# The modulation groups behind the first are made beside the attention instead of beside the branch projections

## The chip, the cores and the metric

The kernel runs on one core of one Trainium2 chip, as one program. The metric is device time in microseconds, from runs of the whole program. Engines are called PE (TensorE, matrix products), DVE (VectorE), ACT (ScalarE), POOL (GpSimd) and SP (the queue that issues nearly all loads).

## The reference, cut to what matters

Two layers act on 256 latent and 256 context tokens of 1024 features, all in float32. Of each layer:

```python
mod = jax.nn.silu(c) @ w_mod[l] + b_mod[l]          # latent; mod_c from c_ctx for the context
sh1, sc1, g1, sh2, sc2, g2 = jnp.split(mod[:, None, :], 6, axis=-1)
y_lat, y_ctx = token_mixers(x_lat * (1 + sc1) + sh1, x_ctx * (1 + csc1) + csh1, ...)
x_lat = layer_norm(alpha * x_lat + g1 * y_lat, ln1_g[l], ln1_b[l])
f_lat = expert_choice_ffn(x_lat * (1 + sc2) + sh2, ...)
x_lat = layer_norm(alpha * x_lat + g2 * f_lat, ln2_g[l], ln2_b[l])
```

`w_mod[l]` is 1024 x 6144. The token mixer has four branches: A, a gated delta rule over chunks of tokens in two directions; B, a difference of two softmax maps; C, grouped-query attention; D, attention with a window and a sink. Each branch's output is multiplied by `w_br`, gated by a sigmoid of 1024 logits per token, summed, and multiplied by `w_out`. The feed-forward has 16 experts that each choose 32 tokens per stream; its weights are 16 x 3 matrices of 1024 x 1024 per layer. The second layer computes latent tokens only behind its keys and values.

## The kernel before, in words

**Modulation.** The six modulation vectors of a layer are made in three groups of two. `mod(l, g)` (L220) is a generator. For each of eight blocks k of 128 rows it loads 128 x 2048 weights (1 MB) by `wload` from SP into one of the three buffers of the pool `wp`, and issues four products (L237) of 128 x 32 by 128 x 512, one for each strip of 32 rows of the PSUM tile `ps_mod`; the eight blocks add up there. The four products stand under `tc.high_priority()`. It yields after each block. After the eighth, the sums are copied, transposed (`ps_mt`, L245) and added to the biases. `ps_mod` is one of the two tiles of the PSUM pool `pa`, from which the attention's scores (`score_ps`), layer 0's state products of the scan and later sums also come. Group (0, 0) is made at the start. Groups (0, 1), (0, 2) and (1, 0) belong to layer 0's mixer, (1, 1) and (1, 2) to layer 1's; their results are used first behind the merge of the branches (gates and norms) and in the next layer.

**Mixer.** `run` takes the steps of `ORDER = "PMBIV"`: P projects branch A and convolves, M makes A's chunk matrices, B projects the three attention branches (`bcd_project`, seven groups of 256 columns: a 1 MB load from `w_in`, a split of each weight into a high and a low part on ACT, DVE and POOL, and three passes of products per token tile into `ps_n`, at L311 to L313), I inverts A's triangles (`a_invert`: a long run on DVE, then products `ps_y` L655 and `ps_z`), V prepares values. Then come A's scan over eight steps, the attention of D, C and B in eight units (`attention`), the gate logits of the branches in `SPILL` (`gates`, `ps_gate`, ended by a tanh on ACT, L1123), the merge with the other branches' gates, the output projection, and the experts (`moe`). Weight loads of `w_mod`, `w_in` (branch and gate), `w_br` and `w_out` all go through `wp`.

**What sets the order.** Nobody writes the order on the engines by hand. A planner lays out every engine's instructions before the run, by a model of their costs: an instruction is placed when its operands and a buffer are free by that model, and among those ready the one that stands earlier in the program goes first (products under `high_priority` before all others). An instruction far down in the program can so be placed early. At run time each queue keeps that order and waits by semaphores.

In step B the generators take turns:

```python
def all_mods():
    it = (x for m in mods for x in self.mod(*m))
    while next(it, True) is None:
        for _ in range(2):
            next(it, None)
        yield
```

One turn is three blocks; `all_of(all_mods(), self.bcd_project(l, bp))` puts one turn ahead of each projection group. Layer 0 has 24 blocks in eight turns, layer 1 has 16 in six.

Of the kernel before, what the change touches and what calls it, by code (L numbers as in the profile page):

```python
# [27 lines left out]
# columns of the packed constants  # L28
# [57 lines left out]
# rows of the packed per-layer vectors (each of 128 elements)  # L86
R_BMOD, R_L1G, R_L1B, R_L2G, R_L2B, R_CONV, R_C, R_CC, NROW = 0, 48, 56, 64, 72, 80, 110, 118, 126
# columns of the packed per-layer small vectors
# [3 lines left out]
class Net:  # L92
# [16 lines left out]
    def rsqrt(self, out, x, n, tag, scale=1.0, eps=EPS):  # L109
        """out[128, n] = (x * scale + eps) ** -0.5"""  # L110
# [12 lines left out]
    def wload(self, src, shape, pool=None):  # L123
        """one streamed weight tile [128, a, b]"""
        w = (pool or self.wp).tile([P, 2048], F32, tag="w", name="w")
        v = w[:, :shape[0] * shape[1]].rearrange("p (a b) -> p a b", a=shape[0])
        self.nc.sync.dma_start(v, src)
        return v

    def split(self, w, n):  # L130
        """hi/lo parts of a streamed weight tile [128, 8, n]: lists over k of [128, n]"""
# [13 lines left out]
    def hilo(self, h, x, w, j):  # L145
        """w = h + x, h of 12 bits"""
# [8 lines left out]
    def rowbcast(self, dst, col):  # L155
        """dst [128, 1024] (every partition) = the vector held as columns col [128, 8]; two vectors: in turns of 32 partitions"""
# [16 lines left out]
    def setup(self):  # L173
# [36 lines left out]
        # silu of both conditioning vectors, padded to a column tile  # L210
# [9 lines left out]
    def mod(self, l, g):  # L220
        """modulation vectors 2g and 2g+1 of layer l, as columns"""
        nc = self.nc
        ps = self.pa.tile([P, 512], F32, tag="s", name="ps_mod")
        for k in range(8):
            src = self.a["w_mod"][l, k * P:(k + 1) * P, g * 2048:(g + 1) * 2048]
            if (l, g) == (0, 0) and k % 2:
                # at the start the weights' parts lend their tiles
# [27 lines left out]
    def all_of(*gens):  # L255
        """what the generators do, in turns"""
# [10 lines left out]
    def make_h(self, src, scl, shf):  # L267
        """src [128, 4 tiles, 1024] natural -> self.hp, transposed; scl/shf[w]: [128, 8] columns"""
# [24 lines left out]
    def h_tile(self, t):  # L293
        """both parts of the activations of token tile t: lists over k of [128, 128]"""
# [5 lines left out]
    def mm_h(self, ps, wh, wl, n0):  # L300
        """ps [128, 512 - n0] = weights.T @ activations of the tokens from n0 on"""
# [5 lines left out]
    def mm3(self, ps, lh, ll, rh, rl, nk=8):  # L307
        """ps = sum over k of (lh+ll).T @ (rh+rl), in three passes"""
# [7 lines left out]
    def a_inputs(self, l, st):  # L316
        """the projections for the decays, natural"""
# [9 lines left out]
        # the transposed keys' tile serves as scratch  # L327
# [8 lines left out]
    def a_project(self, l, st):  # L336
        """short convolution over q, k, v"""
# [5 lines left out]
        # natural k, v [tok, t, (h d)]; q is needed for a while only  # L343
# [4 lines left out]
        # transposed: [d, h, tok]  # L348
# [5 lines left out]
        def conv_tile(ci, hi, lo, c0):  # L354
            n0 = 256 if (ci < 2 and l == 1) else 0       # queries of the context are not needed
# [18 lines left out]
            # twice the silu; the factor is taken out where the result is scaled  # L374
# [19 lines left out]
        # l2 norms (of twice the silu)  # L394
# [23 lines left out]
    def a_gates(self, l, st):  # L418
        """log decays, their cumulative sums and the factors made of them"""
# [4 lines left out]
        # tiles that are filled later on serve as scratch  # L424
        Nm = A["N"] = pl.tile([P, 32, 64], F32, name="a_N")       # stack = (t, d, h)
# [16 lines left out]
        # log1p(e) = 2 atanh(s), s = e / (2 + e) <= 1/3  # L442
# [14 lines left out]
        # half of beta, for v carries a factor of two; beta itself for k  # L457
# [4 lines left out]
        # cumulative sums along the chunks, in the order of each scan: rows (head), tokens along the row;  # L462
        # the backward scan's tokens are reversed within their tile
# [11 lines left out]
        # G and G_last - G  # L475
# [10 lines left out]
        # as columns: [tok, (G, G_last - G), t, (d h)]  # L486
# [13 lines left out]
        # exp(G_last) on the partitions of the state: [d, (dir, chunk in the scan's tiles), h]  # L500
# [7 lines left out]
        # the backward rows once more, in the order of the tokens  # L508
# [6 lines left out]
        # exp(G), exp(G_last - G); beta exp(G)  # L515
# [13 lines left out]
    def a_mats(self, l, st):  # L529
        """per chunk: -(beta k k^T decay) (lower triangles) and (q k^T decay)^T"""  # L530
# [6 lines left out]
        pT = A["pT"] = pl.tile([P, 8 * nq, 64], F32, name="a_pT")      # stack = (query tile, d, h)  # L537
        nb = p1.tile([P, 4, 8], F32, name="a_nb")
        nc.vector.tensor_scalar_mul(nb, bt.rearrange("p t d h -> p t (d h)"), -1.0)
        for t in range(4):  # L540
# [16 lines left out]
            # row of -beta for the backward direction  # L557
# [27 lines left out]
    def a_invert(self, l, st):  # L585
        """R[s, c] = ((I - N)^-1)^T for the forward direction, (I - N)^-1 for the backward one"""
# [9 lines left out]
        # one 32 x 32 block per partition: F[(rb, s), j, i] = N[i, j]  # L596
        F = p1.tile([P, 32, 32], F32, tag="i_F", name="i_F")
        nc.vector.transpose(F, Dg.rearrange("p s j -> p j s"))
        T = p1.tile([P, 32, 32], F32, name="i_T")          # T[r, k], row-major
# [6 lines left out]
        def view(ap, off, dims):  # L606
            """ap: [128, n] flat; dims: (step, count)"""
# [3 lines left out]
        for r in range(1, 16):  # L611
            # rows 16 b + r, b = 0, 1
            i0 = view(Ff, r, [(16 * 33, 2), (0, r), (32, r)])                 # N[16b+r, 16b+q]  (b, k, q)
            i1 = view(Tf, 0, [(16 * 33, 2), (1, r), (32, r)])                 # T[16b+q, 16b+k]
# [3 lines left out]
        # T21 = T22 N21 T11 for the halves of 16  # L618
        Y = p1.tile([P, 16, 16], F32, name="i_Y")          # Y[j, i] = (T22 N21)[i, j]
        for i0, ni, nm in ((0, 8, 8), (8, 4, 16), (12, 4, 16)):  # L620
            # (i, j, m): T[16+i, 16+m] * N[16+m, j]
# [6 lines left out]
        for k0, nk in ((0, 8), (8, 8)):  # L628
            # (i, k, j): Y[i, j] * T[j, k], j >= k0
# [466 lines left out]
    def attention(self, l):  # L1096
# [3 lines left out]
        for i, (_, unit) in enumerate(jobs):  # L1100
            cur, nxt = nxt, (jobs[i + 1][0]() if i + 1 < len(jobs) else None)
            unit(*cur)
# [650 lines left out]
```

## Time and profile before

| | us |
|---|---|
| timed runs, median of 3 | 2188.01 (2185.98 to 2192.87) |
| profiled execution, span from first to last instruction | 2171.3 |
| PE busy in the span | 1849.2 (85%) |
| PE weight loads busy | 1199.7 (55%) |
| DVE busy | 955.9 (44%) |
| ACT busy | 503.8 (23%) |
| POOL busy | 350.6 (16%) |
| bytes moved | 553.92 MB, mean 255 GB/s |

For the profiled execution the span is what is given; its total outside the span is not recorded. Busy times of an engine are unions over its instructions. Matrix products are pipelined, so that one that shows 0.28 us may follow the one before it by 0.12. An instruction's idle time ahead of it is put down to what released it last. The PE clock is shown as a share of 2.4 GHz; its two levels are 1.2 and 2.4 GHz, and a stretch's number is a mean.

### The profile page before, as it was taken

The page shows a single profiled execution, that of the slowest core. Times are in us where ns is not written, and L with a number is a line of the kernel's source. Part 1 is how long each engine was busy: PE and PEld are TensorE (multiplying, and loading weights), DVE is VectorE, ACT ScalarE, POOL GpSimd, SP SyncE. Part 2 cuts the span into 40 slices and gives each one's busy share as a digit, 9 for nine tenths or more (in the row PEclk, how much of TensorE's full clock was granted, in tenths as well). Part 3 has the DMA queues.
Part 4 walks back from the last instruction along what each step waited for, and adds up shares of the span by engine and source line. Part 5 has one row for each costly group of instructions (what it writes and reads, how often), then busy time and mean ns, then how long its engine had stood idle before and what let it go on. Part 6 is the DMA issues. An engine that isn't in the chain of part 4 may idle for free. (4 is left out here: it accounts for less than half of the span.)

```text
span 2171.3 us, 33547 instructions
## 1 busy us (share of the span) xinstructions
PE 1849.2 (85%) x13730; PEld 1199.7 (55%) x13730; DVE 955.9 (44%) x2126; ACT 503.8 (23%) x1038; POOL 350.6 (16%) x380
## 2 busy tenths in 40 slices
PE   6898899989999899988797898899899886676665
PEld 2676778867788555322222376778889542232221
DVE  3859547773226424221121486977755430110102
ACT  2332116752222111000000332246543100000000
POOL 1151330012532000000000125330264000000000
PEclk9999999998999899999999999999999896777767
DMA  7445413117333589999999655302487899999996
GB/s 290 161 170 194 156 36 108 54 59 260 110 126 137 211 335 350 409 409 409 409 409 409 239 194 182 130 24 96 134 271 265 323 408 409 409 409 409 409 409 274
DMA packets 200181, 553.92 MB, mean 255 GB/s; under 512 B 16222, under 2 KB 83164, under 8 KB 194396
## 3 DMA queue, kind: packets, MB, share of 16 engines
q1 hardware_dynamic: 190960, 538.56, 65.6%
q10 hardware_dynamic: 9068, 13.23, 1.7%
q8 instruction: 108, 1.77, 0.3%
q14 instruction: 45, 0.37, 0.1%
HBM read 541.25 MB, written 10.49 MB: 254 GB/s over the span
## 5 line engine op out<-in xcount | busy, mean ns | idle before, releaser
L1458 PE MATMUL ps_gu<-w,xgT 128*32 128x256 f32 (+1 forms) x1632 | 241.2, 533 | 69.5 <-DMA w<-in_w_gate_e_dram 35.5
L149 POOL TENSOR_TENSOR wl<-w,wh 128x1024 fp32r<-128x1024 f32 x62 | 154.1, 2486 | 884.1 <-DMA w<-in_w_in_dram 504.2
L1458 PE MATMUL ps_gu<-we,xgT 128*32 128x256 f32 (+1 forms) x1440 | 204.1, 512 | 38.8 <-DMA we<-in_w_up_e_dram 24.3
L1458 PEld LDWEIGHTS ps_gu<-w,xgT 128*32 128x32 f32 (+1 forms) x1632 | 78.8, 134 | 212.1 <-issue 83.0
L1500 DVE TENSOR_TENSOR y<-ps_dn,g2r 32x512 f32<-32x512 f32 (+1 forms) x128 | 70.9, 554 | 259.0 <-PE ps_dn L1489 257.5
L311 PE MATMUL ps_gate<-hh,wh 128*128 128x512 f32 (+1 forms) x512 | 179.8, 351 | 0.4 <-ACT wh L148 0.4
L313 PE MATMUL ps_gate<-hh,wl 128*128 128x512 f32 (+1 forms) x512 | 179.5, 351 | 0.0
L312 PE MATMUL ps_gate<-hl,wh 128*128 128x512 f32 (+1 forms) x512 | 179.4, 350 | 0.0
L148 ACT CAST wh<-w 128x1024 fp32r<-128x1024 f32 x124 | 129.6, 1049 | 179.2 <-PE ps_gate L312 77.3
L1458 PEld LDWEIGHTS ps_gu<-we,xgT 128*32 128x32 f32 (+1 forms) x1440 | 63.1, 128 | 167.3 <-DMA we<-in_w_up_e_dram 62.1
L1489 PE MATMUL ps_dn<-w,eaT 128*32 128x256 f32 (+1 forms) x896 | 119.1, 522 | 32.5 <-DMA w<-in_w_down_e_dram 26.8
L1468 ACT ACTIVATE eth<-ps_gu 128x512 f32<-128x512 f32 (+1 forms) x32 | 15.7, 491 | 518.4 <-PE ps_gu L1458 518.4
L311 PE MATMUL ps_n<-wh,hh 128*128 128x256 f32 x400 | 116.7, 292 | 7.3 <-DVE c_v L861 3.1
L312 PE MATMUL ps_n<-wl,hh 128*128 128x256 f32 x400 | 115.8, 290 | 8.2 <-POOL wl L149 8.2
L1471 DVE SCALAR_TENSOR_TENSOR eac<-eth,ps_gu 128x512 f32<-128x512 f32 (+1 forms) x32 | 17.7, 554 | 235.1 <-PE ps_gu L1458 235.1
L149 DVE TENSOR_TENSOR wl<-w,wh 128x1024 fp32r<-128x1024 f32 x62 | 85.9, 1385 | 72.9 <-ACT wh L148 72.6
L313 PE MATMUL ps_n<-wh,hl 128*128 128x256 f32 x400 | 115.9, 290 | 0.0
L1489 PE MATMUL ps_dn<-we,eaT 128*32 128x256 f32 (+1 forms) x640 | 93.4, 512 | 15.6 <-DMA we<-in_w_down_e_dram 11.1
L311 PEld LDWEIGHTS ps_gate<-hh,wh 128*128 128x128 f32 x512 | 99.4, 194 | 11.4 <-ACT wh L148 0.8
L312 PEld LDWEIGHTS ps_gate<-hl,wh 128*128 128x128 f32 x512 | 99.2, 194 | 10.8
L313 PEld LDWEIGHTS ps_gate<-hh,wl 128*128 128x128 f32 x512 | 99.0, 193 | 10.8 <-DVE wl L149 0.2
L1470 DVE SCALAR_TENSOR_TENSOR eth<-eth,ps_gu 128x512 f32<-128x512 f32 (+1 forms) x32 | 17.7, 554 | 193.3 <-ACT eth L1468 193.3
(453 smaller groups left out, 3591.2 us busy)
## 6 DMA issues: line engine op xcount, KB each, us to landing
w<-in_w_gate_e_dram SPq DMA_DIRECT2D x75, 1024.0 KB, 13.2
w<-in_w_down_e_dram SPq DMA_DIRECT2D x72, 1024.0 KB, 12.7
w<-in_w_up_e_dram SPq DMA_DIRECT2D x62, 1024.0 KB, 13.9
we<-in_w_up_e_dram SPq DMA_DIRECT2D x120, 512.0 KB, 13.4
w<-in_w_in_dram SPq DMA_DIRECT2D x54, 1024.0 KB, 5.2
we<-in_w_down_e_dram SPq DMA_DIRECT2D x108, 512.0 KB, 14.0
we<-in_w_gate_e_dram SPq DMA_DIRECT2D x96, 512.0 KB, 13.9
w<-in_w_mod_dram SPq DMA_DIRECT2D x44, 1024.0 KB, 5.0
```

Source lines behind the costliest of these rows:

```text
L148: nc.scalar.copy(h, w)
L149: (nc.gpsimd if j else nc.vector).tensor_tensor(x, w, h.bitcast(F32), op=OP.subtract)
L311: nc.tensor.matmul(ps, lh[k], rh[k], start=(k == 0), stop=False)
L312: nc.tensor.matmul(ps, lh[k], rl[k], start=False, stop=False)
L313: nc.tensor.matmul(ps, ll[k], rh[k], start=False, stop=(k == nk - 1))
L1458: nc.tensor.matmul(ps[M * q:M * q + M, :NF], xg[e // 4][:, 2 * kk + k, e % 4, :], w[k][:, q * NF:(q + 1) * NF], start=(kk == 0 and k == 0) ...
L1468: nc.scalar.activation(th, pss[0][:, :NF], AF.Tanh, scale=0.5)
L1470: nc.vector.scalar_tensor_tensor(th, th, 1.0, pss[0][:, :NF], op0=OP.add, op1=OP.mult)
L1471: nc.vector.scalar_tensor_tensor(ac, th, 0.5, pss[1][:, :NF], op0=OP.mult, op1=OP.mult)
L1489: nc.tensor.matmul(py[M * q:M * q + M, :NF], av[:, fc % nj, fc // nj, :], w[k][:, q * NF:(q + 1) * NF], start=(fc == 0), stop=(fc == 7))
L1500: nc.vector.tensor_tensor(ys[w][32 * e4:32 * e4 + 32, q * NF:(q + 1) * NF], py[o:o + 32, :NF], g2r[o:o + 32, q * NF:(q + 1) * NF], op=OP.mult)
```

## The change

The call of `all_mods()` leaves step B. The generator is handed to `attention`, which takes one turn (three blocks) after each of its eight units, and what is left behind the last. The products, loads and their sizes stay the same. The diff also strips comments and docstrings, which are left out here.

```diff
-    def attention(self, l):
+    def attention(self, l, fill):
         B = self.B
         jobs = self.attn_gqa(l, 3, B["dqk"], B["dv"], True) + self.attn_gqa(l, 2, B["cqk"], B["cv"], False) + self.attn_diff(l)
         nxt = jobs[0][0]()
         for i, (_, unit) in enumerate(jobs):
             cur, nxt = nxt, (jobs[i + 1][0]() if i + 1 < len(jobs) else None)
             unit(*cur)
+            next(fill, None)
+        self.all_of(fill)
...
                     elif step == "B":
-                        self.all_of(all_mods(), self.bcd_project(l, bp))
+                        self.all_of(self.bcd_project(l, bp))
...
-                self.attention(l)
+                self.attention(l, all_mods())
```

## Rows read from the trace of the kernel before

**Rows 1.** the page: 40 slices, transfer rate, modulation loads (KB, us to landing).

```profile
PE   6898899989999899988797898899899886676665
GB/s 290 161 170 194 156 36 108 54 59 260 110 126 137 211 335 350 409 409 409 409 409 409 239 194 182 130 24 96 134 271 265 323 408 409 409 409 409 409 409 274
...
w<-in_w_mod_dram SPq DMA_DIRECT2D x44, 1024.0 KB, 5.0
```

**Rows 2.** stretches: length, each engine's busy time (instructions), PE clock, DMA share, GB/s.

```profile
123.00:255.00 132.00, 119.74 (x1037) 99.52 (x1035) 94.61 (x180) 31.26 (x54) 41.48 (x80) 0.99 0.54 185
255.00:280.00 25.00, 17.88 (x345) 13.52 (x344) 13.46 (x26) 5.64 (x11) 12.10 (x15) 0.80 0.17 54
280.00:345.00 65.00, 63.77 (x680) 50.13 (x680) 33.53 (x73) 14.93 (x25) 16.67 (x19) 1.00 0.23 78
345.00:470.00 125.00, 119.74 (x804) 101.70 (x804) 105.37 (x337) 93.51 (x277) 7.68 (x3) 0.99 0.15 52
1320.00:1340.00 20.00, 14.82 (x127) 10.32 (x124) 8.04 (x18) 2.73 (x3) 8.23 (x19) 0.74 0.49 167
1480.00:1562.00 82.00, 73.06 (x591) 66.55 (x589) 67.45 (x166) 52.06 (x127) 17.21 (x7) 0.99 0.35 119
```

**Rows 3.** tile ps_gate (min/median/max ns, first and last start), then ACT's timeline.

```profile
L1123 ACT ACTIVATE th<-ps_gate x16: 576/598/612, 277.6 to 500.3; 128x512 f32<-128x512 f32 x16
...
342.44 0.59 ACT L1123 ACTIVATE th<-ps_gate 128x512 f32<-128x512 f32 x1
...
382.43 0.60 ACT L1123 ACTIVATE th<-ps_gate 128x512 f32<-128x512 f32 x1
...
408.89 0.60 ACT L1123 ACTIVATE th<-ps_gate 128x512 f32<-128x512 f32 x1 [0.30 <-PE ps_gate L313]
```

**Rows 4.** DVE's timeline (start, us): the inversion's last copies, layers 0 and 1.

```profile
213.91 0.28 DVE L666 COPY a_N<-i_Tn 32x256 f32<-32x256 f32 x1
...
1400.55 0.28 DVE L666 COPY a_N<-i_Tn 32x256 f32<-32x256 f32 x1
```

**Rows 5.** tiles ps_n (layer 0) and ps_y (layers 0, 1): first and last start.

```profile
L313 PE MATMUL ps_n<-wh,hl x224: 277/281/469, 123.6 to 254.8; 128*128 128x256 f32 x112
...
L655 PE MATMUL ps_y<-i_Rn,a_N x128: 191/224/257, 255.4 to 269.8; 32*32 32x32 f32 x128
...
L655 PE MATMUL ps_y<-i_Rn,a_N x128: 191/224/257, 1415.0 to 1426.8; 32*32 32x32 f32 x128
```

**Rows 6.** PE's waits (total, times, longest us), 40 to 340, 1205 to 1440.

```profile
PE ps_z L677 <- DVE i_YT L658: 7.1, 1, 7.1
...
PE ps_mod L237 <- DMA w<-in_w_mod_dram: 3.6, 4, 1.6
...
PE ps_mod L237 <- DMA w<-in_w_mod_dram: 7.4, 3, 5.2
```

**Rows 7.** PE's timeline: the long wait ahead of a modulation product, layer 1.

```profile
1330.12 1.93 PE L237 MATMUL ps_mod<-w,silc 128*32 128x512 f32 x8 [5.18 <-DMA w<-in_w_mod_dram]
```

**Rows 8.** modulation products, 40 to 500 (busy, mean ns, idle), then 123 to 260.

```profile
L237 PE MATMUL ps_mod<-w,silc 128*32 128x512 f32 x192 | 26.4, 624 | 3.7 <-DMA w<-in_w_mod_dram 3.6
...
L237 PE MATMUL ps_mod<-w,silc x128: 592/605/617, 124.6 to 236.9; 128*32 128x512 f32 x128
```

**Rows 9.** SP's queue (start, us from first to last of the merged issues).

```profile
220.17 8.61 SPq L127 DMA_DIRECT2D w<-in_w_mod_dram  x3
234.02 91.58 SPq L127 DMA_DIRECT2D w<-in_w_in_dram  x6
```

**Rows 10.** PE's timeline: two products of 512 columns in a row.

```profile
86.04 0.39 PE L311 MATMUL ps_a<-hh,wh 128*128 128x512 f32 x1
86.27 0.40 PE L312 MATMUL ps_a<-hl,wh 128*128 128x512 f32 x1
```

**Rows 11.** score tiles ps_sc: layer 0's first products; layer 1's row maxima.

```profile
L1019 PE MATMUL ps_sc<-kA,qT x32: 277/388/500, 348.0 to 403.4; 128*128 128x256 f32 x16, 128*128 128x512 f32 x16
...
L974 DVE TENSOR_REDUCE mx<-ps_sc x32: 666/680/692, 1434.8 to 1543.4; 128x1 f32<-128x512 f32 x32
```

## The prediction

> **What bounds the kernel now.** The span is 2171.3 us. First the forty slices [rows 1]: TensorE (PE) is busy nearly throughout, and the transfers run at 409 GB/s only in slices 17 to 22 and 33 to 39, where the experts' weights stream. So each layer has a mixer stage, bound elsewhere, and a feed-forward stage paced by transfers. The change touches the mixer; the feed-forward starts when that ends, so I carry a shift over whole.
>
> Then the stages [rows 2], with idle read as length minus busy. From 123 to 255 (attention projections, with modulation steps between) PE is idle for 12.3 of 132 us, in the inversion 7.1 of 25, in the scan 1.2 of 65, in layer 0's attention 5.3 of 125. PE stays full in scan and attention because a reserve is drawn on: the gate products of the spilled branches, later in the program, are pulled forward. Their first tile of sixteen is evicted at 277.6, the last at 500.3, the sixth at 342.44 [rows 3].
>
> Third, what the scan waits for. The inversion's VectorE part ends with the copy at 213.91, but its first product, ps_y, starts at 255.4, behind the last projection product of 254.8 [rows 4, 5]. PE takes the projections first. In layer 1 the copy is at 1400.55 and ps_y at 1415.0. So the projections' PE time holds up branch A by up to 41 and 14 us.
>
> Fourth, the waits [rows 6]: modulation products waited 3.6 us for transfers in layer 0 and 7.4 in layer 1, one wait 5.2 long, before the product at 1330.12 [rows 7]; around it, 1320 to 1340, the granted clock averages 0.74 [rows 2], a part of the time at 1.2 instead of 2.4 GHz. ps_z waited 7.1 us for VectorE, and the clock from 255 to 280 is 0.80.
>
> **What the change removes.** A step is one 1 MB load and eight records (four products, each recorded twice): 192 records, 24 steps, busy 26.4 us, or 1.1 each [rows 8]. 16 of layer 0's steps (128 records) lie between 124.6 and 236.9: 17.6 us of PE, and I count all 3.6 of waits with them. The eight earlier ones lie in the convolution; I count half of them, 4 us, as felt, because PE waits for VectorE there. The projections would end at 254.8 - 17.6 - 3.6 - 4 = 230. Layer 1 has 16 steps, 17.6 us, with its 7.4 of waits.
>
> **Where the steps go.** Not simply into the attention. The planner runs an instruction as soon as operands and a buffer are free, earlier program lines first; the gate weights, which stand behind the attention, were loaded from 234.02 on, directly behind the last modulation load of the 220.17 row [rows 9]. On that queue the modulation loads now come after the seventh projection load and before the gate loads, and their products keep the highest priority. They need one of three weight buffers. A projection group takes (131 - 17.6 - 3.6)/7 = 15.7 us, and its buffer is free about when its products begin, so the buffers of the last three groups come free some 47, 31 and 16 us before the projections end. A buffer turns round in about 7 us (5.0 to land [rows 1], 1.1 for the products, about 1 for the issue; an estimate from those rows): 2, 4 and 5 steps, 11 in all. They push the projections' end to 230 + 12 = 242. ps_y then starts 13 us earlier, with the inversion's copy (213.91) no limit.
>
> The 13 steps left run at the rate of transfers: 1.05 MB take 2.6 us at 409 GB/s, or 3.6 at the 290 of the first slice, where the first group's weights were streamed and the start is counted in [rows 1]; I take 2.8, nearer the first, 36 us, until about 278. So they fill inversion and scan, and the gate loads start near 275 instead of 234. Queued behind them on SP are those gate loads and nothing else that is urgent; ScalarE's and GpSimd's splits of gate weights follow. A gate tile is 24 products, 0.23 us apart in the same 512-column shape [rows 10]: 5.6 us. By the attention's start (13 us earlier than before), three tiles instead of six would be done, at one in 14 us as before; 17 us of them fall later, where PE is also full. The step count is constant, so moving is worth nothing by itself; only idle PE time and half clock are won.
>
> **Layer 0, the sum.** Waits for modulation loads: -3.6. The 7.1 of ps_z, which steps can fill: -7.1 to 0, taken -5, for steps arrive one in 2.8 us. Half clock, 25 x (1 - 0.80) = 5.0: -5 to 0, taken -3.5. New waits on streamed loads, a kind that the trace does not show: nearest are 3.6 in 24 steps and 7.4 in 16 (0.15 to 0.46 each), so 2 to 6 for 13 steps, or less than nothing if slack meets them; I take +3, with the scan's state products in it, which share a PSUM pool with the modulation sums. The hole in the reserve: gates filled 6 x 5.6 = 34 of the 86 us up to 342, 39%, and steps fill 1.1 in 2.8, the same; the first gate's load and split after them, +2; between 0 and 34. Sum -7.
>
> **Layer 1, the sum.** Waits -7.4, half clock 20 x (1 - 0.74) = 5.2, taken -4; new waits +2. In this layer all scores use the two PSUM tiles of one pool, and a modulation sum holds one of them for its eight loads. The attention's first scores may meet the last steps for some 20 us: 0 to 6 (32 scores lie between 1434.8 and 1543.4 [rows 11], one in 3.4 us), taken +1.5. Sum -8.
>
> Moved waits and the rest cancel. Span 2171.3 - 15 = 2156. No total of the profiled execution is given; the median of the timed runs, 2188.0, is 16.7 above the span, and I keep that: 2173.
>
> **A rule against PE as the bound.** In attention PE shows 119.7 busy of 125, its weight loads 101.7 [rows 2]. The Trainium skill ("Perfetto Trace Analysis", Identifying the Most-Contended Engine) says that matmul busy time does not measure headroom and that weight-load time does. By it layer 0 leaves 125 - 101.7 = 23 us of room for the steps, which is rival 3. The trace speaks against it so far: gates lay ready, yet one tile took from 382.43 to 408.89 to come through.
>
> **Rivals.** 1: the work merely changes place. New waits eat what the old ones give back; within 0.3%, about 2188. For it: PE idle in scan and attention is small. Against: the 5.2 us wait and the two half-clock stretches are whole gaps.
>
> 2: slower. The moved loads take the three weight buffers early, but their sums wait for their place among the scores; then no gate weights can be loaded through scan and half the attention. Six tiles, 34 us, that filled the time up to 342 are missing, PE idles there and pays them after the attention: +34 - 3.6. Layer 1 pays up to 10 of its 8 x 24 x 0.115 = 22 us of gates (half the columns) and gets 12 back. 2188 + 30 - 2 = 2216. It decides if the last modulation load of layer 0 is issued after the first score (348.0 in [rows 11]). For it: one buffer pool serves all, and loads stand ahead of the gates. Against: in [rows 9] instructions far behind the attention were pulled up without waiting for their turn, and nothing else wants the score pool before the scan.
>
> 3: attention has room, because only the weight loads bind PE, 101.7 of 125 us. Then steps and displaced gates vanish into it: layer 0 -23 - 3.6, layer 1 82 - 66.6 = 15 [rows 2] and 7.4: -49, 2139. For: 15 us or more of free weight-load time in each. Against: the gate tile above.
>
> **Chances.** Forecast 0.48, rival 1 0.22, rival 2 0.20, rival 3 0.10. The forecast's own range is 2160 to 2183. The range reaches toward rivals 2 and 3 and covers the hole's price up to half: 2152 to 2208. 0.3%, 6.6 us, is about what a measurement tells from no change: faster 0.55 (nearly all of the forecast, and rival 3), same 0.23, slower 0.22.
>
> **What would show it.** Modulation products from about 185 on, none between 70 and 160; ps_y near 242 and, in layer 1, near 1400; no 5 us wait for a modulation load as at 1330; the first gate tile evicted after 290, with about thirteen tiles left when the attention starts, against ten; the clock in the inversion above 0.80. The prediction is wrong if the products run during the scores, if scan or attention gains more than 10 us of idle PE, or if ps_y hardly moves.

## The result and the profile after

The kernel after takes 2275.9 us (median of 4 runs, 2268.0 to 2276.2) against 2187.0 (2182.3 to 2192.9) for the kernel before: ratio 1.041, 95% interval 1.038 to 1.044. The forecast was 2173, its range ended at 2208. The profiled span grew from 2171.3 to 2274.3, by 103 us; it is 89 in the medians, because the profiled execution of before was among its shorter ones. Places in the span are compared by the profiles, totals by the medians.

The page of after, forty slices: PE's busy tenths, its granted clock, the transfer rate [rows 1].

```profile
PE   6898769889899799989787788789889896676665
PEclk9989659999999899999999998969999897786877
GB/s 277 56 57 56 20 20 252 188 171 150 231 111 118 170 250 342 399 409 409 410 409 409 288 64 49 75 67 237 163 248 258 255 409 409 409 409 408 409 409 260
```

Slices 2 to 6, 57 to 341 us, move 20 to 57 GB/s where before moved 36 to 194. PE's tenths fall to 7 and 6 in slices 5 and 6, and the clock with them. The experts' slices are as they were. So the loss is in the mixers, and in layer 0 it begins with a lack of transfers. The next view, windows, shows the scan and the attention of layer 0 [rows 2] (length, busy us of PE, PEld, DVE, ACT, POOL, PE's clock, DMA share, GB/s):

```profile
255.00:320.00 65.00, 45.05 (x535) 41.86 (x532) 28.24 (x68) 3.66 (x8) 9.75 (x16) 0.50 0.00 1
320.00:330.00 10.00, 6.10 (x24) 4.44 (x24) 3.08 (x6) 5.38 (x12) 0.00 (x0) 0.50 0.27 105
330.00:470.00 140.00, 125.71 (x863) 88.44 (x864) 101.60 (x343) 87.69 (x267) 2.68 (x1) 0.95 0.56 198
```

From 255 to 330 the clock is 0.50, the lower level of 1.2 GHz for the whole stretch; PE is idle for 20 of the 65 us up to 320, in which next to nothing is moved (1 GB/s). SP's queue says why (start, us from first to last of the merged issues; it answers [rows 9]):

```profile
198.25 30.13 SPq L127 DMA_DIRECT2D w<-in_w_mod_dram  x3
...
346.46 22.83 SPq L127 DMA_DIRECT2D w<-in_w_mod_dram  x8
...
382.42 24.02 SPq L127 DMA_DIRECT2D w<-in_w_mod_dram  x8
...
435.58 10.53 SPq L127 DMA_DIRECT2D w<-in_w_mod_dram  x5
449.17 17.47 SPq L127 DMA_DIRECT2D w<-in_w_in_dram  x4
```

Three modulation loads take the three weight buffers by 228. The fourth can start only when a buffer comes free, at 346, and all gate loads stand behind the last one: the first gate weights are asked for at 449.17, at 234.02 before. What kept the buffers is in the tiles: the modulation sums, the gate tiles evicted [rows 3], layer 0's row maxima, and layer 1's [rows 11].

```profile
L237 PE MATMUL ps_mod<-w,silc x192: 592/592/617, 345.3 to 455.7; 128*32 128x512 f32 x192
...
L1125 ACT ACTIVATE th<-ps_gate x16: 586/599/600, 473.7 to 564.7; 128x512 f32<-128x512 f32 x16
...
L974 DVE TENSOR_REDUCE mx<-ps_sc x64: 404/548/692, 334.2 to 460.8; 128x1 f32<-128x256 f32 x32, 128x1 f32<-128x512 f32 x32
...
L974 DVE TENSOR_REDUCE mx<-ps_sc x32: 665/682/693, 1497.5 to 1633.0; 128x1 f32<-128x512 f32 x32
```

And layer 0's row maxima before:

```profile
L974 DVE TENSOR_REDUCE mx<-ps_sc x64: 399/544/693, 348.9 to 461.9; 128x1 f32<-128x256 f32 x32, 128x1 f32<-128x512 f32 x32
```

The first sum starts at 345.3, 14 us after the first score (331.4), though its first three loads had been issued by 228. The sums got their tile of the scores' pool in the order of the program, among the scores (with a tile from another pool, in e1 below, they start at 235.7). The gates, of which six tiles were evicted by 342 before, all come after 473. The attention, from its first maximum to its last, takes 126.6 us (before 113.0) in layer 0 and 135.5 (108.6) in layer 1.

The end of each layer's mixer, by the last product of the branch outputs (before, then after; min/median/max ns, first and last start):

```profile
L312 PE MATMUL ps_br<-ol,bh x64: 387/397/792, 463.4 to 653.7; 128*128 128x512 f32 x64
...
L312 PE MATMUL ps_br<-ol,bh x64: 278/283/579, 1547.1 to 1656.9; 128*128 128x256 f32 x64
```

```profile
L312 PE MATMUL ps_br<-ol,bh x64: 387/397/628, 564.8 to 717.9; 128*128 128x512 f32 x64
...
L312 PE MATMUL ps_br<-ol,bh x64: 278/283/415, 1651.2 to 1755.7; 128*128 128x256 f32 x64
```

Layer 0 ends 64.2 us later. From there to the same place in layer 1 it is 1037.8 us against 1003.2, 34.6 more, and 4.2 come after. These two lengths are the yardstick below. Kernels whose layer 0 is untouched end it between 652.7 and 654.0. The 64.2 can be split once more, by the windows from 40 us to that end (before, then after):

```profile
40.00:653.90 613.90, 569.60 (x3999) 454.51 (x4000) 359.23 (x786) 224.45 (x478) 170.77 (x183) 0.96 0.38 128
```

```profile
40.00:718.10 678.10, 599.90 (x3999) 488.93 (x4000) 357.41 (x787) 226.98 (x478) 171.39 (x183) 0.89 0.35 116
```

The same 3999 products are busy for 30.3 us more, at a mean clock of 0.89 instead of 0.96, and idle time grows from 44.3 to 78.2 us, by 33.9.

### The profile page after: what moved, and what is told of

The parts are those of the page before. It is cut to its first block, busy times and chain, and to the rows that moved or that the text cites. A ratio compares the mean times of both kernels' runs of the same rounds, so it can differ in the third digit from the quotient of the medians.

```text
span 2274.3 us, 33570 instructions
## 1 busy us (share of the span) xinstructions
PE 1899.0 (83%) x13730; PEld 1251.2 (55%) x13730; DVE 957.7 (42%) x2126; ACT 506.1 (22%) x1038; POOL 350.9 (15%) x380
## 5 line engine op out<-in xcount | busy, mean ns | idle before, releaser
L311 PE MATMUL ps_gate<-hh,wh 128*128 128x512 f32 (+1 forms) x512 | 175.2, 342 | 1.3 <-ACT wh L148 1.3
L1460 PEld LDWEIGHTS ps_gu<-we,xgT 128*32 128x32 f32 (+1 forms) x1440 | 62.7, 128 | 171.9 <-DMA we<-in_w_up_e_dram 66.2
L312 PE MATMUL ps_n<-wl,hh 128*128 128x256 f32 x400 | 121.2, 303 | 19.1 <-POOL wl L149 19.1
L311 PE MATMUL ps_n<-wh,hh 128*128 128x256 f32 x400 | 121.2, 303 | 10.4 <-DVE c_v L861 3.7
L1472 DVE SCALAR_TENSOR_TENSOR eth<-eth,ps_gu 128x512 f32<-128x512 f32 (+1 forms) x32 | 17.8, 555 | 196.6 <-ACT eth L1470 196.6
## 6 DMA issues: line engine op xcount, KB each, us to landing
we<-in_w_up_e_dram SPq DMA_DIRECT2D x120, 512.0 KB, 13.6
```

The costliest lines, as they stand in the source:

```text
L311: nc.tensor.matmul(ps, lh[k], rh[k], start=(k == 0), stop=False)
L312: nc.tensor.matmul(ps, lh[k], rl[k], start=False, stop=False)
L1460: nc.tensor.matmul(ps[M * q:M * q + M, :NF], xg[e // 4][:, 2 * kk + k, e % 4, :], w[k][:, q * NF:(q + 1) * NF], start=(kk == 0 and k == 0) ...
L1472: nc.vector.scalar_tensor_tensor(th, th, 1.0, pss[0][:, :NF], op0=OP.add, op1=OP.mult)
```

## The experiments

All at a glance. "First gate" is the first gate product of layer 0, "layer 0" its mixer's end against 653.7, "layer 1" the way from there to layer 1's against 1003.2; us, of one profiled execution each. The ratio is of the times, to before. What a profile differs by beyond the two columns comes behind layer 1's mixer (-0.1 to 11.5 us). In e14, whose layer 1 is that of before, layer 1 differs by 3.2; differences of that size say nothing.

| kernel | median | ratio (95%) | first gate | layer 0 | layer 1 |
|---|---|---|---|---|---|
| before | 2182 to 2187 | 1 | 256.6 | 0 | 0 |
| after | 2275.9 | 1.041 (1.038 to 1.044) | 460.6 | +64.2 | +34.6 |
| e1 sums in the other PSUM pool | 2210.9 | 1.014 (1.011 to 1.018) | 386.0 | +25.7 | +5.7 |
| e2 behind the projections | 2206.4 | 1.012 (1.009 to 1.016) | 299.4 | +14.3 | +19.6 |
| e6 own load buffer | 2213.7 | 1.015 (1.012 to 1.018) | 230.1 | +2.9 | +23.0 |
| e8 e1 and e6 together | 2247.4 | 1.029 (1.025 to 1.033) | 409.7 | +48.9 | +26.0 |
| e4 before, no gate reserve | 2227.6 | 1.022 (1.019 to 1.025) | 259.3 | +48.8 | -7.3 |
| e17 after, scan filled | 2270.1 | 1.040 (1.036 to 1.045) | 459.6 | +62.5 | +34.1 |
| e7 before, no later groups | 2148.8 | 0.984 (0.980 to 0.988) | 230.3 | -29.7 | +1.1 |
| e5 layer 1 alone | 2216.4 | 1.018 (1.015 to 1.022) | 255.6 | -1.0 | +37.7 |
| e11 layer 1, other PSUM pool | 2196.8 | 1.008 (1.005 to 1.011) | 256.2 | +0.3 | +17.8 |
| e10 layer 0, own load buffer | 2202.6 | 1.009 (1.005 to 1.012) | 238.4 | +7.7 | +23.2 |
| e13 before, own load buffer | 2177.9 | 0.998 (0.995 to 1.001) | 250.0 | -13.6 | +11.9 |
| e15 layer 0, own buffer, control | 2203.5 | 1.011 (1.007 to 1.015) | 235.1 | +7.6 | +16.3 |
| e14 in turns with the gates | 2178.1 | 0.999 (0.997 to 1.001) | 230.3 | -4.3 | +3.2 |
| e9 reserve in layer 0 alone | 2178.6 | 0.999 (0.997 to 1.002) | 256.4 | +0.2 | -2.5 |
| e16 e9, e13 and e14 together | 2199.3 | 1.008 (1.005 to 1.011) | 230.5 | +10.4 | -1.0 |

**What holds the gate weights up: the sums' place (e1), the place in the program (e2), the buffers (e6), both (e8).**

e1:

```
-        ps = self.pa.tile([P, 512], F32, tag="s", name="ps_mod")
+        pool, tag = ((self.pm, "m"), (self.pa, "s"))[(l, g) == (0, 0)]
+        ps = pool.tile([P, 512], F32, tag=tag, name="ps_mod")
```

> The kernel after, with one thing changed: the sums of the later modulation groups stand in the other PSUM pool, the one of the branches' projections, and not in the pool of the scores. Theory 1 (the sums wait for their place in the order of the scores' pool, and through that wait their first three loads hold all three weight buffers, so that no gate weights can be loaded): layer 0's sums are formed before 300 us, gate products stand in the scan again from about 260 to 300 us on, the granted clock between 255 and 320 us is above 0.85, and the time comes back to 2165 to 2200. Theory 2 (the 26 us of moved products and their loads are too much for the attention wherever they stand in it): 2255 to 2290, as the kernel after. Theory 3 (layer 1's scores have one tile in place of two while a sum is open): about 35 us of the kernel's 89 come back in layer 1 even if layer 0 stays as it is.

e2 (the attention gets an empty list of steps):

```
                         self.all_of(self.bcd_project(l, bp))
+                        self.all_of(all_mods())
...
-                self.attention(l, all_mods())
+                self.attention(l, iter(()))
```

> The later modulation groups are made directly behind the attention branches' projections, alone and not in turns with anything; nothing of them is left in the attention. Their sums stay in the scores' pool. Theory 1: no sum waits behind a score, so the loads pass and the gate weights come in time: 2165 to 2200, with the scan between 255 and 320 us above a granted clock of 0.85. This is also the order that the forecast of 2173 described. Theory 2: the products are out of the attention too, so that it forecasts the same; what tells the two apart is whether the scan's clock and the gates' begin come back by the same edit.

e6:

```
-        self.wp = self.pool("wts", bufs=self.NW)
+        self.wp = self.pool("wts", bufs=self.NW - 1)
+        self.wmp = self.pool("wtm", bufs=1)
...
-                w = self.wload(src.unsqueeze(1), (1, 2048))
+                w = self.wload(src.unsqueeze(1), (1, 2048), pool=(self.wp if (l, g) == (0, 0) else self.wmp))
...
-            order2 = order + [self.wp] * self.NW + ...
+            order2 = order + [self.wp] * (self.NW - 1) + [self.wmp] + ...
```

> The kernel after, with the three weight buffers shared out: the loads of the later modulation groups have one buffer of their own, all other loads of that pool the other two. The sums keep their place among the scores. If the held buffers are the whole cause (theory 1, second half), the gate weights pass the waiting loads, gate products begin near 260 us, the scan's granted clock is above 0.85, and the time is 2185 to 2210. If the place of the sums in the scores' pool costs by itself (the attention 15 us longer in layer 0, 27 us in layer 1, as the trace of after shows them), 2215 to 2240. Theory 2 (the moved work): 2255 to 2290, for all of it is still in the attention.

e8 is e6 with e1's three lines.

> The kernel after with both waits taken away: the later groups' loads have one of the three weight buffers to themselves, and their sums stand in the projections' PSUM pool. Theory 1 (two waits make up the loss: in layer 0 the held buffers, in layer 1 the sum's place in the scores' pool) now gives both layers back: layer 0's last merge product within 6 us of before's 653.9, layer 1 from its first projection to its last merge product 355 to 368 us (357 in before, 395 in after, 384 with the own buffer alone, 368 with the other PSUM pool alone), total 2180 to 2200. Theory 2 (the moved 26 and 18 us of products cost their own time once nothing hides them): no better than the two single edits, 2205 to 2220.

SP's queue of e1, and under it, from the timelines of DVE, PE and ACT, the last split of the first gate weights, the transposes of the first sum, the copy of the second sum and the first gate product:

```profile
198.28 112.45 SPq L127 DMA_DIRECT2D w<-in_w_mod_dram  x24
313.88 1.24 SPq L127 DMA_DIRECT2D w<-in_w_in_dram  x2
...
326.97 2.63 DVE L149 TENSOR_TENSOR wl<-w,wh 128x1024 fp32r<-128x1024 f32 x1 [0.67 <-ACT wh L148]
...
384.69 0.60 PE L246 MATMUL ps_mt<-const,mrow 128*128 128x128 f32 x4
...
385.33 0.59 ACT L243 COPY mrow<-ps_mod 128x512 f32<-128x512 f32 x1 [0.84 <-PE ps_mt L246]
...
385.97 0.50 PE L312 MATMUL ps_gate<-hh,wh 128*128 128x512 f32 x1
```

SP's queue of e2, then of e6:

```profile
194.11 88.34 SPq L127 DMA_DIRECT2D w<-in_w_mod_dram  x24
285.31 50.83 SPq L127 DMA_DIRECT2D w<-in_w_in_dram  x5
```

```profile
314.10 0.38 SPq L127 DMA_DIRECT2D w<-in_w_in_dram  x1
...
334.08 0.33 SPq L127 DMA_DIRECT2D w<-in_w_mod_dram  x1
```

SP's queue of e8, and under it the split of the first gate weights on ACT, the copy of the second sum and the first gate product:

```profile
195.07 31.52 SPq L127 DMA_DIRECT2D w<-in_w_in_dram  x3
...
246.32 88.91 SPq L127 DMA_DIRECT2D w<-in_w_mod_dram  x10
...
399.75 22.90 SPq L127 DMA_DIRECT2D w<-in_w_mod_dram  x4
...
237.67 1.04 ACT L148 CAST wh<-w 128x1024 fp32r<-128x1024 f32 x1 [0.37 <-PE ps_n L315]
...
404.60 0.59 ACT L244 COPY mrow<-ps_mod 128x512 f32<-128x512 f32 x1
...
409.74 0.48 PE L313 MATMUL ps_gate<-hh,wh 128*128 128x512 f32 x1
```

In e2 all 24 loads pass by 282, the gates begin at 299.4, and 14.3 are lost. In e6 the gate loads are in front, since they need not wait for a buffer that a waiting sum holds. The first gate product comes at 230.1, the last of the sixteen tiles is evicted at 477.2, the clock from 255 to 320 is 1.00, and layer 0 loses 2.9.

In e1 the sums no longer wait for scores, and all 24 loads pass by 311. I had expected gates by 300; they come at 386.0, and layer 0 still loses 25.7. The gate weights, behind the modulation loads, are asked for at 313.88, 80 us later than before. But they are split by 330, and the first product waits 56 us more for a tile of its own PSUM pool, where the sums now stand too. The first sum is copied out at 262, and its transposes, which stand behind the attention's first three units in the program and take a tile of a pool that these use too, run at 384.69 only. They free the one buffer for copied rows, the second sum is copied at 385.33, and with the tile that this frees the gates start at 385.97.

In e8, from which I expected both layers back, gates start at 409.7 and layer 0 loses 48.9. The modulation loads go one at a time through their one buffer, 7 to 10 us apart, up to 423. But the first gate weights do not stand behind them: three gate loads are issued from 195 to 227, and the first of them is split by 246. Again the second sum's tile is what comes late, with its copy at 404.60.

So a moved sum holds up the gates in two ways: in after through the weight buffers, while their loads stand behind its own, and in e1 and e8 through the tiles of their pool. e6 has neither, and its gates are the earliest of the four. Whether in after the order of the queue or the held buffers themselves kept the gate weights away no run separates, for e6 changes both. Theory 2, that the 26 us of products are too much for the attention wherever they stand in it, forecast 2255 or more; e6, with most of them there, took 2213.7.

**Is the lost reserve enough? e4 and e17.**

```
-        self.SPILL = ((0, 3), (3,))
+        self.SPILL = ((), ())
```

> The kernel before, with the modulation as it was there, but no gates made ahead: every gate is made where its branch is merged. Theory 1 says that what the change costs is the lost gate reserve, and so this kernel must lose much of the same without any change to the modulation: the scan of layer 0 at a granted clock of 0.5 to 0.6, the attention no longer than before (about 115 us from the first score to the last), layer 0 35 to 55 us later, layer 1 10 to 25 us later, 2235 to 2265 in all. Theory 2 (the attention's load is the cause): the gates cost about the same later as earlier, 2187 to 2205.

e4's windows, scan and what follows:

```profile
255.00:320.00 65.00, 53.14 (x780) 43.95 (x778) 33.07 (x68) 10.20 (x19) 25.59 (x32) 0.76 0.08 26
320.00:350.00 30.00, 18.07 (x162) 16.35 (x163) 14.63 (x32) 7.17 (x13) 3.12 (x3) 0.50 0.11 31
```

With the modulation untouched, the reserve's absence costs layer 0 48.8 us, three quarters of after's loss; the clock falls to 0.50 here too, though later (two gate tiles were still pulled forward, and evicted by 346), and the attention is as long as before (113.9). Layer 1 was expected to lose 10 to 25 and gained 7.3. The clock by itself is e17, the kernel after with this in layer 0's scan:

```
+            if l == 0:
+                pf = self.pm.tile([P, 512], F32, tag="m", name="ps_fill")
+                for _ in range(6):
+                    nc.tensor.matmul(pf[:, :256], self.c("ident"), r.rearrange("p h n -> p (h n)"), start=True, stop=True)
```

> The kernel after with six matrix products more in each of the eight steps of layer 0's scan (128x256, into a PSUM tile that nobody reads): work that only fills the matrix engine. If the half clock of the scan in the kernel after is due to the missing gate products, the granted clock between 255 and 320 us rises above 0.85, the state products go from 311 to 218 ns, the scan gets 6 to 10 us shorter in spite of the added work, and the total falls by 6 to 14 us, to 2262 to 2270. If the clock has another cause, the scan gets 8 to 16 us longer (48 products, 0.2 to 0.4 us each) and the total 2284 to 2292.

Windows of after, then of e17, and e17's state products:

```profile
255.00:300.00 45.00, 35.29 (x424) 32.83 (x422) 17.90 (x42) 1.86 (x5) 9.75 (x16) 0.50 0.00 1
```

```profile
255.00:300.00 45.00, 39.16 (x478) 33.47 (x478) 16.48 (x39) 1.86 (x5) 5.89 (x10) 0.90 0.01 1
```

```profile
L727 PE MATMUL ps_s<-S,a_qT x112: 218/218/365, 248.3 to 302.2; 64*64 64x64 f32 x112
```

The clock comes back (0.84 from 255 to 320, short of the 0.85 expected) and the state products take 218 ns, 311 in after. So the half clock there follows from the missing gate products. But the scan, 54 us from its first to its last product of this group, is no shorter than after's 52 (254.9 to 306.8), and the total, 1.040, can't be told from after's 1.041. What the clock gave, the filler took: work that nobody wants did not replace here the work that is wanted anyway. (e17's projections also end earlier, at 229.3 against 237.8, though its edit does not touch them.)

**What the work cost where it was: e7.** Before without the later groups (no loads, no products; their columns hold a constant).

```
-                mods = ((0, 1), (0, 2), (1, 0)) if l == 0 else ((1, 1), (1, 2))
+                mods = ()
```

> The kernel before without the later modulation groups: neither their loads nor their products run, and their columns hold a constant. It gives the price of this work where before has it, among the projections. If the projections hide it there (their matrix engine is idle for part of the stage anyway), 2170 to 2190, and then whatever it costs elsewhere is new cost; if it is paid there in full (26 us in layer 0, 18 in layer 1), 2140 to 2150, and a move to a place that hides it could have won up to 40 us. The trace of after, whose projections are without it, ended them 17 us earlier in layer 0 and 4 us sooner in layer 1; by that, 2160 to 2170, with this range the likeliest.

e7's projection products of layer 0, and the last products of its branch outputs (of layer 0's, the last eight):

```profile
L314 PE MATMUL ps_n<-wh,hl x224: 276/280/471, 112.7 to 229.0; 128*128 128x256 f32 x112
...
L313 PE MATMUL ps_br<-ol,bh x8: 397/397/398, 602.3 to 624.0; 128*128 128x512 f32 x8
...
L313 PE MATMUL ps_br<-ol,bh x64: 278/282/420, 1520.2 to 1628.3; 128*128 128x256 f32 x64
```

The whole work is worth 1.6% of the time (1.2 to 2.0%). All of it lies in layer 0, where the mixer ends 29.7 us sooner, about the 26.4 that its products are busy [rows 8]. In layer 1, without the 17.6 us of products, the way is 1.1 longer: there before had them for nothing, and a move had nothing to gain.

**Layer 1: e5 and e11.** The change in layer 1 alone; in e11 with its sums in the projections' pool, by e1's edit.

```
-                        self.all_of(self.bcd_project(l, bp))
+                        self.all_of(*([] if l == 1 else [all_mods()]), self.bcd_project(l, bp))
...
-                self.attention(l, all_mods())
+                self.attention(l, all_mods() if l == 1 else iter(()))
```

> The change in layer 1 alone, as the diff has it: sums in the scores' pool, all three weight buffers shared. Theory 1 (the sums take a score's tile and hold the buffers in each layer by itself): about the 35 us that layer 1 lost in the kernel after, 2210 to 2222. If layer 1's loss there was only the echo of a late layer 0, 2180 to 2195.

> The change in layer 1 alone, with its two sums in the projections' PSUM pool. Without the work of the later groups at all, layer 1 took as long as with it (1004 us from layer 0's last merge product to layer 1's, against 1003), so that in before layer 1's groups are hidden in full; moved, they have to be paid somewhere, and no version of layer 1 that moves them can gain. Theory 1: of the 35 us all but 5 to 12 are back, 2186 to 2196. If the pool is not what cost (the held buffers alone are), 2205 to 2220.

SP's queue of e5, then of e11, from 1380 on:

```profile
1390.80 91.65 SPq L127 DMA_DIRECT2D w<-in_w_mod_dram  x9
...
1516.96 8.09 SPq L127 DMA_DIRECT2D w<-in_w_in_dram  x3
```

```profile
1380.80 75.77 SPq L127 DMA_DIRECT2D w<-in_w_mod_dram  x15
1461.26 25.39 SPq L127 DMA_DIRECT2D w<-in_w_in_dram  x4
```

Layer 1 loses by itself, 37.7 us, and its loss is no echo of layer 0's. Moving the sums away from the scores gives back 20 of them. Of the 17.8 left I had expected 5 to 12. The gate weights are still asked for at 1461 only, some 50 us behind the last projection product (1411.6). The second sum, whose last product starts at 1468.3, is copied out of the gates' pool at 1518.1. And the work that had been free may now be paid. How the 17.8 divides no run tells.

**The own buffer's control: e10, e13, e15.** e10 has the change in layer 0 alone (e5's edit with 0 for 1) and e6's buffers, the one for the three groups of layer 0 only; e15 lets layer 1's groups use it too; e13 is before with e6's buffers.

> The change in layer 0 alone, with one weight buffer of its own for the three groups that are moved; layer 1 makes its two groups among the projections, as before. With the own buffer in both layers, layer 0 lost nothing (its last merge product at 656.8 against 653.9), and the 26 us after it came from layer 1. Theory 1: 2180 to 2195, no gain and no loss, because the projections' 17 us come back as an attention that is longer by as much. If instead the loss of layer 1 in that run came from the shared-out buffers and not from the moved sums, layer 1 loses here too: 2205 to 2215.

> The control for the two runs with an own load buffer: the kernel before, modulation where before has it, with one weight buffer for the later groups' loads and two for the rest. In the run with the change in layer 0 only, layer 1 (whose code is that of before) took 17 us longer from its first projection to its last merge product. If two buffers in place of three are the reason, 2195 to 2210 here; if it was the change in layer 0, 2178 to 2192.

> The change in layer 0 alone with the own load buffer, once more, but now layer 1's two groups (made among the projections, as before) use that buffer too, as in the control with shared-out buffers in the kernel before (2178). Theory 1 in its present form, that layer 0's whole loss is the order of the loads (gate weights held behind loads that wait): layer 0 ends within 10 us of before and layer 1 takes no longer than in the control, 2178 to 2192. If the sums among the scores cost by themselves although the gates are made in time (the attention took 160 us from first score to last maximum in the two earlier runs of this kind, against 113), 2195 to 2210.

Row maxima of layer 0's attention, in e13, then in e15:

```profile
L975 DVE TENSOR_REDUCE mx<-ps_sc x64: 398/548/692, 345.1 to 459.9; 128x1 f32<-128x256 f32 x32, 128x1 f32<-128x512 f32 x32
```

```profile
L975 DVE TENSOR_REDUCE mx<-ps_sc x64: 403/548/692, 326.5 to 486.0; 128x1 f32<-128x256 f32 x32, 128x1 f32<-128x512 f32 x32
```

Products of the branch outputs, in e13, then in e15:

```profile
L313 PE MATMUL ps_br<-ol,bh x64: 387/397/628, 485.2 to 640.1; 128*128 128x512 f32 x64
```

```profile
L313 PE MATMUL ps_br<-ol,bh x64: 387/397/628, 489.4 to 661.3; 128*128 128x512 f32 x64
```

Windows of that attention, e13, then e15:

```profile
345.10:459.90 114.80, 111.59 (x758) 95.15 (x758) 96.73 (x319) 87.43 (x259) 7.13 (x3) 1.00 0.15 51
```

```profile
326.50:486.00 159.50, 155.25 (x1009) 113.63 (x1007) 101.14 (x333) 96.23 (x272) 11.84 (x5) 1.00 0.51 179
```

The control corrects what e6 seemed to say. Shared-out buffers alone end before's layer 0 13.6 us sooner and make layer 1 11.9 longer, for reasons that no run here shows; in total they are level. Against that control, e15's layer 0 is 21.2 us late (+7.6 against -13.6) with its gates in time. So of after's 64.2 us, 43 to 61 go with the late gates (64.2 less these 21.2, or less e6's 2.9); e4, with no reserve at all, loses 48.8.

e15 starts the attention 18.6 us earlier than e13 and needs 159.5 us for it in place of 114.8. That is not waiting. PE is idle for 4.2 of the 159.5 us; it does there what e13 does elsewhere, modulation products (busy for 21.3 us) and more of the gates (68.1 against 48.2). By 486 all sixteen gate tiles are evicted in both, and the branch outputs begin 4.2 us late (489.4 against 485.2). The other 17.0 us arise behind that, for they take 171.9 us in place of 154.9; the last two modulation loads are issued there, at 500.6 and 510.3. Why that part is longer no run shows. e15's total, 1.011, is in the range that I had put on a price of the sums among the scores, but the trace does not show the price there. Of e10's 23.2 in layer 1, some 7 go with e15's edit, 12 with the control's.

**Versions: e14, e9, e16.** e14 makes layer 0's groups in turns with the gates of the reserve, behind the attention in the program, their sums in the projections' pool; layer 1 as before:

```
-    def gates(self, l, br):
+    def gates(self, l, br, fill):
...
                 self.thd[br, cc] = d
+            next(fill, None)
...
+                fill = all_mods() if l == 0 else iter(())
                 for b in self.SPILL[l]:
-                    self.gates(l, b)
+                    self.gates(l, b, fill)
+                self.all_of(fill)
```

> Another place for layer 0's three groups: in turns with the gates that are made ahead, one group's step behind each gate group, with their sums in the projections' PSUM pool; layer 1 as before. The loads then stand between the gates' loads in the queue instead of in front of them, and no sum waits for a score. The projections of layer 0 end 17 to 26 us earlier; the 26 us of products are paid in the scan and the attention in place of gates. Theory 1 (what decides is whose weights stand first in the queue; the work itself only changes place): 2178 to 2196, neither a gain nor a loss of more than 0.5%. Theory 2: 2205 and more. A gain, 2155 to 2175, would say that scan and attention have idle time that the gates left unused.

e9 has SPILL = ((0, 3), ()).

> The kernel before with the gate reserve in layer 0 only; layer 1 makes its gates in the merge. Without any reserve layer 0 lost 48 us, and layer 1 was 11 us shorter from its first projection to its last merge product (346 against 357). If that holds, 2170 to 2180, faster than before; if the 11 us were due to layer 1's later start, 2183 to 2195. Theory 1 in its plain form, that gates made ahead pay in both layers by filling the scan, expects a loss of 10 to 25 us: 2195 to 2210.

> The three edits that were level or slightly ahead, together: the groups of layer 0 in turns with the gates made ahead, no gate reserve in layer 1, one weight buffer of its own for the later groups' loads. Each alone was at 0.998 to 0.999 of before. If their layer-wise gains add up (layer 0 5 to 14 us earlier, layer 1 3 to 11 us shorter), 2160 to 2175; if they fill the same idle time, 2176 to 2186; if the single buffer holds the gates' weights up, as it did with the sums in the projections' pool, 2195 to 2230.

e14's gate products of layer 0:

```profile
L312 PE MATMUL ps_gate<-hh,wh x256: 387/394/774, 230.3 to 647.8; 128*128 128x512 f32 x128
```

e14 is the move without its waits: gates from 230.3 on, the projections' last product at 228.9, and no gain, 0.999 (0.997 to 1.001). The work changes place and costs there what it cost here. e9 is level as well, so that layer 1's reserve is worth nothing that can be measured. Together with the own buffer they lose 0.8%, as I had allowed for a single buffer with the sums in the projections' pool. No version here beats before.

## Why the prediction was wrong

**What bounds the kernel** and **what the change removes** held for layer 0. The projections were to end at 230 without the steps; they did at 229.0 in e7 and 228.9 in e14. In after they end at 237.8, and ps_y, forecast near 242, came at 238.0 ([rows 5] had 255.4). That was luck: the 242 had eleven steps pulled in among the projections, and there were none. The 9 us between e7 and after stand beside a granted clock of 0.71 from 123 to 150, 0.92 in e7. (One sum there is a step short: 47 us hold six turns of 7, not five. It moves the 242 by 1 us.) In layer 1 the removal was sized at 17.6 + 7.4 us and was worth nothing (e7: 1.1 longer): busy products and waits counted as path there, though they lay beside other work.

**Where the steps go** is the step that failed. "Not simply into the attention": they went exactly there. I let the planner pull the steps forward as it had pulled the gates [rows 9], and noted that the sums share the scores' pool, but took a tile of that pool to be free for them. The pool's tiles are given in program order, and the first sum stood behind scores: it began at 345.3, its loads kept the three buffers, and the gate weights were asked for 215 us later than before (449.17 against 234.02). The row that I leaned on showed loads pulled ahead of their turn, not a PSUM tile.

**The hole in the reserve** was the term that carried this: +2, "between 0 and 34". e2 made nearly the order that I forecast (loads from 194, four gate tiles by the first score where I had three), and there layer 0 lost 14.3 instead of gaining 7, 21 us off. Windows, before, then e2:

```profile
255.00:320.00 65.00, 57.03 (x842) 44.04 (x841) 33.38 (x70) 10.97 (x22) 23.89 (x31) 0.92 0.14 46
```

```profile
255.00:320.00 65.00, 56.66 (x657) 38.74 (x650) 25.73 (x66) 9.13 (x17) 16.98 (x20) 0.76 0.61 205
```

With the steps in the place of gates PE was as busy, but the granted clock fell to 0.76, and from the last projection product to the first score it took 106.3 us (93.2 before). From the last maximum to the layer's end it took 203.7 (191.8). So the hole cost far more than +2; how much of the 21 us it makes by itself no run separates. In after, with no gate before 460, the layer lost 64 in all. I gave a step that fills PE the worth of a gate that fills it; but the gates not made are still to be made later, and the steps in their place did not keep the clock up.

**Layer 1, the sum**, -8, came out as +34.6. Moving the sums out of the scores' pool gave back 20 of e5's 37.7, where I had put the collision of scores and sums at +1.5. The gate weights also come 56 us sooner by that edit (1461 against 1517), so that the 20 are not the collision alone.

**Rival 2** had the mechanism, place and test right: the last modulation load was issued at 446, after the first score at 331.4. Its price of 34 us for layer 0 left out that the same products are busy for longer at the lower clock (30.3 of the 64.2), and its -2 for layer 1 was wrong in sign. At 2216 it was still 60 short. **Rival 1** is what a move without waits does (e14).

**Rival 3** took the attention to have some 23 us of room. It went by a rule of the Trainium skill ("Perfetto Trace Analysis", Identifying the Most-Contended Engine), that headroom on PE is judged by MFU, the share of peak arithmetic, and by weight-load time, not by product time. For weight-load time the trace of this stage does not agree: in e15 some 41 us more of modulation and gate products than in e13 made the attention 44.7 us longer, although its weight loads were busy for only 95.2 of 114.8 us in e13.

**What stays open**: how layer 1's last 17.8 us divide; why an own load buffer shifts 12 to 14 us from one layer to the other in before; and why e15's branch outputs take 17.0 us longer than e13's.

## What to carry to other kernels

A moved piece of work waits for things and holds things. Ask of each load what it waits for and which loads stand behind it in its queue. Ask of each PSUM tile, given in program order, how long it is held until it is copied out, and who needs the next one: here the gates waited 56 us for it in e1 and 164 in e8, with their weights ready. Before moving work, take it out once: the time without it tells about what a move can win, and here it was 30 us in one layer and nothing in the other. Work drawn forward as filler can be worth much in one layer and nothing in the next (48.8 us in e4, nothing that can be measured in e9), and it is lost as soon as its weights or its tile come late.

## What the runs showed of the hardware

The granted clock stood at 0.50 for the whole of 255 to 330 us in after, which has no gate products between the scan's small ones; with six wider products more per step, into a tile that nobody reads, it was 0.90 from 255 to 300. At the two levels the 64x64 state products show 311 and 218 ns, not double: part of the time that such a product shows does not follow the clock.
